# A second pair of value projections in seven half-sized products, its rows put in order through DRAM

## The chip, the cores and the metric

The kernel runs on one core of one Trainium2 chip. The metric is the time of one execution on the device in microseconds (us); lower is better. A time is the median of several runs; the traces come from one profiled execution each.

## The reference

One layer of a decoder trunk, in float32, for 512 tokens of width 1024. What matters here is the first half, the mixer:

```python
proj = x @ w_in        # (512,1024) @ (1024,9216): q/k/v of three branches and three gates
o_da  = diff_attention(...)            # 4 heads, values da_v: 512 columns, keys in order
o_sb  = stick_breaking_attention(...)  # 8 heads, values sb_v: 512 columns
o_dl  = dilated_attention(...)         # 3 groups x 4 heads, dilation 1, 4 and 16
# values dl_v[0], dl_v[1], dl_v[2]: 512 columns each, for the three groups
merged = sum_i sigmoid(gate_i) * (o_i @ w_branch_i)
x = layer_norm(alpha * x + merged @ w_out)
# then a squared-ReLU MLP and a gated per-layer embedding, and a second layer norm
```

The first dilated group (dilation 1) and the differential attention read their values in the order of the tokens; the second and third dilated groups read every fourth token, so that for them the rows stand in four classes (token number modulo 4).

## The kernel before

**Products.** Each operand is held as two float32r tiles, a rounded high part and the rest (h and l), and a product is three matmuls: h by h, h by l and l by h. The weights stream from DRAM in chunks of 128x1024 float32 (512 KB). A chunk is loaded on the SP queue into one of six raw buffers (line 211), cast to its high part by ACT (line 243), and its low part is a subtraction on DVE (line 245). Six pairs of h and l buffers make the ring; chunks are split up to six ahead of the matmuls, and a chunk's buffers come free when its last matmul is done.

**Items.** All projections stand in one list `items`, in an order that `main_order()` gives. A T item (line 292) makes 128 columns of q or k, transposed, with one chunk and 24 matmuls of 128x512. A V projection (`v_items`, line 488) makes 512 value columns in four items of 24 matmuls each, one for each 128 tokens, with four chunks in all; its four results are copied to SBUF by DVE (line 513). The rows are in the order of the tokens.

**Seven products.** A pair of value projections (`value_pair`, line 441) is a product of a 2x2 block matrix of tokens by input rows with a 2x2 block matrix of weights. It is computed with seven block products in place of eight (the scheme of Strassen and Winograd, p = 1 to 7), each as two half-sized items of 12 matmuls. Products 1, 2 and 3 take the activations as they are: their stationary operand reads every fourth column of `xh` and `xl` (line 364, `2 * th + r::4`), so that the rows come out in classes. Products 4 to 7 take sums of activation blocks, which `value_forms` makes on DVE and splits on ACT and DVE, from a copy of x that is loaded on the POOL queue. On the weight side they take sums of weight chunks. These are made in DRAM by DMA with an accumulating add on the POOL queue (`sum_steps`, lines 1095 and 1097), ahead of time, a few steps for each item: every item adds `size * rate` to a credit, and each whole credit issues one step. Up to four chains of steps run in turn, and a step of a chain needs the one before it landed. Two sums of a pair, for products 7 and 3, are made in place by `then_add`: a DMA on the POOL queue adds a second block onto the raw chunk after it was split for another product (line 176).

**Order around the change.** Behind the stick-breaking items (numbers 0 to 10) come the q and k items of dilated head 0 (11 to 16), two items of head 1, the plain value projection `dl_v` 0 (19 to 22), the other four items of head 1, the six of head 2, the pair `dl_v` 1 and 2 (33 to 46), the plain projection `da_v` (47 to 50), then the q and k of the differential heads and of dilated head 3, up to item 64. The gate and branch products follow, then the output projection and the MLP, all with their own weight sums.

**Attention pieces.** The attention heads are generators. `step()` (line 1937) is called at every item, and once more in the middle of a T or V item, and moves each active head on by one piece: some small matmuls and then work on ACT and DVE. The eight stick-breaking heads go first, two at a time, then dilated heads 0, 1 and 2, and so on. A dilated head ends with its product with the values (lines 1905 and 1910), which needs all three `dl_v`; a differential block needs `da_v` (line 1751). Semaphores are set by the framework from the tiles that an instruction reads and writes; the order of an engine's instructions is in the main the written one, but the framework may put a ready instruction ahead of one that it expects to wait.

Of the kernel before, what the change touches and what calls it, by code (L numbers as in the profile page):

```python
# [10 lines left out]
F32 = mybir.dt.float32  # L11
# [5 lines left out]
S = 512  # L17
# [18 lines left out]
def main_order():  # L36
# [5 lines left out]
    for h in range(4):  # L42
        for g in range(3):
            o += [("T", "dl_q", 4 * g + h), ("T", "dl_k", 4 * g + h)]
            if h == 1 and g == 0:
                o += [("V", "dl_v", g)]
        if h == 2:
            o += [("V", "dl_v", 1), ("V", "dl_v", 2), ("V", "da_v", 0)]
# [7 lines left out]
def trunk(tc, a, out):  # L56
    nc = tc.nc
    es = ExitStack()
    with es:
# [306 lines left out]
        vsum = [[dram.tile([P, 1024], F32, name=f"vsum{m}_{i}") for i in range(2)] for m in range(2)]  # L366
        v_from = [None]

        def load_xr():

            r = {}
            for h in range(2):
                for th in range(2):
                    for kp in range(2):
                        t = slot("xr")
                        i = nc.gpsimd.dma_start(t.rearrange("p (k t) -> p k t", k=2),
                                                xt[:, 4 * h + 2 * kp:4 * h + 2 * kp + 2, 256 * th:256 * th + 256])
# [10 lines left out]
        def value_forms():  # L388

            xr = [slot("xr") for _ in range(8)]  # L390
            for k, t in enumerate(xr):
                i = nc.gpsimd.dma_start(t, xt[:, k, :])
                tc.add_manual_dep(getattr(i, "ins", i), lows[-1].name, mybir.DependencyInfo(
                    mybir.DependencyClass.Sync, mybir.DependencyReason.DATA), reason="not ahead of time")

            def blk(kh, k, th):
                return xr[4 * kh + k].rearrange("p (t c) -> p c t", c=4)[:, 2 * th:2 * th + 2, :]

            def new():
                ts = [slot("fr") for _ in range(2)]  # L400
                return ts, [ts[k // 2].rearrange("p (k c t) -> p k c t", k=2, c=2)[:, k % 2] for k in range(4)]

            def parts(p, ts):
                form(vf, p, ts)
                vf[p] = [[(h[:, r * P:r * P + P], lo[:, r * P:r * P + P]) for r in range(2)] for h, lo in vf[p]]

            def neg_sub(o, i, j):
                nc.vector.scalar_tensor_tensor(o, i, -1.0, j, op0=OP.mult, op1=OP.subtract)

            for _ in range(WAIT):  # L410
                yield
            f7, o7 = new()
            with tc.issue_after(st["low"]):
                for k in range(4):
                    nc.vector.tensor_sub(o7[k], blk(1, k, 1), blk(0, k, 1))
            parts(7, f7)
            yield
            f6, o6 = new()
            with tc.issue_after(st["low"]):
                for k in range(4):  # L420
# [1732 lines left out]
```

## Time and profile before

| | |
|---|---|
| median of 3 runs | 1042.92 us (1042.3 to 1043.47) |
| the profiled execution | 1043.19 us |
| its span in the trace | 1041.0 us |
| granted TensorE clock | 0.998 |
| DMA traffic | 249.21 MB, mean 239 GB/s |

The trace's views are read so: the page gives for each engine the time in which at least one of its instructions was in flight. TensorE's matmuls overlap (a 128x512 matmul shows 389 ns, while the next one starts earlier), so the price of a matmul is the distance between two starts and not its duration. The view of windows gives the busy time of each engine in a stretch of the span, with the share of time that the 16 DMA engines were busy. The timeline lists instructions by start.

### The profile page before, as it was taken

The numbers are of one execution on the slowest core, as the hardware profiler recorded it, in microseconds if no ns is written. First come the engines' busy times: TensorE is split into PE (matmuls) and PEld (weight loads), VectorE is DVE, ScalarE is ACT, GpSimd is POOL, SyncE is SP. The second block draws the span as 40 slices with busy tenths as digits, with TensorE's granted clock in tenths as the row PEclk, the third lists the DMA queues.
The fourth block names the chain that finished last, engine by engine and source line by source line (L and its number), as shares of the span: only waits on it lengthen the run. The fifth ranks groups of instructions, "written<-read, shape, count | busy, mean of one in ns | idle before, by whom it ended". The sixth has DMA issues, their size and how long they took to land.

```text
span 1041.0 us, 15056 instructions
## 1 busy us (share of the span) xinstructions
PE 1031.1 (99%) x5450; PEld 880.1 (85%) x5450; DVE 787.0 (76%) x1408; ACT 593.2 (57%) x1014; POOL 180.0 (17%) x271
## 2 busy tenths in 40 slices
PE   9999999999999999999999999999999999999997
PEld 6888788889888888888888888889999889889886
DVE  6888577769774667779788895798768877877966
ACT  7566445536344545676575743775666556555651
POOL 0003412031211232411011040111111111111001
PEclk9999999999999999999999999999999999999999
DMA  8449978495985999967889795479999999999612
GB/s 308 121 154 271 255 214 197 128 283 142 278 207 206 258 281 294 248 199 202 251 238 230 269 320 197 147 219 331 320 288 316 296 316 314 306 344 286 201 59 81
DMA packets 71323, 249.21 MB, mean 239 GB/s; under 512 B 8809, under 2 KB 9593, under 8 KB 71249
## 3 DMA queue, kind: packets, MB, share of 16 engines
q0 software_dynamic: 32464, 116.21, 44.7%
q1 hardware_dynamic: 38208, 131.13, 35.2%
q8 instruction: 43, 0.70, 0.3%
q10 hardware_dynamic: 576, 0.92, 0.2%
q14 instruction: 32, 0.25, 0.1%
HBM read 246.10 MB, written 98.59 MB: 331 GB/s over the span
## 4 chain that ended last, share of the span: by engine, by line
PE 94%; DVE 2%; ACT 2%; issue 1%; DMA 0%; POOL 0%; DVEq 0%; POOLq 0%
PE mm L87 10%; PE mm L88 10%; PE mm L89 10%; PE at L1261 4%; PE at L1262 4%; PE at L1263 4%; PE at L599 3%; PE at L601 3%; PE at L600 3%; PE mm L496 2%; PE mm L498 2%; PE mm L497 2%; PE at L89 1%; PE at L87 1%; PE at L88 1%; PE at L761 1%
## 5 line engine op out<-in xcount | busy, mean ns | idle before, releaser
L243 ACT CAST wh<-raw 128x1024 fp32r<-128x1024 f32 x257 | 268.7, 1049 | 241.1 <-PE mm L88 133.6
L245 DVE TENSOR_TENSOR wl<-raw,wh 128x1024 fp32r<-128x1024 f32 x257 | 312.5, 1222 | 112.2 <-ACT wh L243 110.9
L87 PE MATMUL mm<-xhT,wh 128*128 128x512 f32 x302 | 120.0, 397 | 0.0
L89 PE MATMUL mm<-xhT,wl 128*128 128x512 f32 x302 | 118.3, 392 | 0.0
L88 PE MATMUL mm<-xlT,wh 128*128 128x512 f32 x302 | 118.2, 391 | 0.0
L87 PE MATMUL mm<-x1hT,wh 128*128 128x256 f32 x256 | 73.8, 288 | 0.0
L1261 PE MATMUL at<-wh,hh 128*128 128x512 f32 x188 | 73.7, 392 | 0.0
L1262 PE MATMUL at<-wl,hh 128*128 128x512 f32 x188 | 73.7, 392 | 0.0
L1263 PE MATMUL at<-wh,hl 128*128 128x512 f32 x188 | 73.1, 389 | 0.0
L88 PE MATMUL mm<-x1lT,wh 128*128 128x256 f32 x256 | 72.2, 283 | 0.0
L89 PE MATMUL mm<-x1hT,wl 128*128 128x256 f32 x256 | 71.8, 283 | 0.0
L89 PEld LDWEIGHTS mm<-xhT,wl 128*128 128x128 f32 x302 | 56.8, 188 | 12.0
L87 PEld LDWEIGHTS mm<-xhT,wh 128*128 128x128 f32 x302 | 56.8, 188 | 11.3 <-issue 0.4
L88 PEld LDWEIGHTS mm<-xlT,wh 128*128 128x128 f32 x302 | 56.8, 188 | 10.5
L87 PEld LDWEIGHTS mm<-x1hT,wh 128*128 128x128 f32 x256 | 48.8, 190 | 4.8 <-ACT up L1195 2.9
L88 PEld LDWEIGHTS mm<-x1lT,wh 128*128 128x128 f32 x256 | 48.9, 191 | 1.5
L89 PEld LDWEIGHTS mm<-x1hT,wl 128*128 128x128 f32 x256 | 48.6, 191 | 0.0
L1095 POOL DMA_DIRECT2D usum<-in_wu_dram x32 | 28.5, 928 | 103.1 <-DVE wl L245 38.7
L1095 POOL DMA_DIRECT2D dsum<-in_wd_dram x28 | 25.5, 933 | 100.2 <-DVE wl L245 33.3
L1263 PEld LDWEIGHTS at<-wh,hl 128*128 128x128 f32 x188 | 35.3, 188 | 7.6
L1261 PEld LDWEIGHTS at<-wh,hh 128*128 128x128 f32 x188 | 35.5, 189 | 6.0
L1262 PEld LDWEIGHTS at<-wl,hh 128*128 128x128 f32 x188 | 35.5, 189 | 5.6
(601 smaller groups left out, 2686.4 us busy)
## 6 DMA issues: line engine op xcount, KB each, us to landing
usum<-in_wu_dram POOLq DMA_DIRECT2D x48, 512.0 KB, 9.2
dsum<-in_wd_dram POOLq DMA_DIRECT2D x42, 512.0 KB, 9.1
raw<-in_wt_dram SPq DMA_DIRECT2D x38, 512.0 KB, 5.7
raw<-usum SPq DMA_DIRECT2D x32, 512.0 KB, 7.8
raw<-dsum SPq DMA_DIRECT2D x28, 512.0 KB, 8.1
raw<-in_wd_dram SPq DMA_DIRECT2D x25, 512.0 KB, 6.5
raw<-in_wu_dram SPq DMA_DIRECT2D x24, 512.0 KB, 7.2
raw<-in_wv_dram SPq DMA_DIRECT2D x18, 512.0 KB, 5.5
```

What stands on the lines that cost most here:

```text
L87: nc.tensor.matmul(ps, wh, xh, start=start, stop=False, skip_group_check=True)
L88: nc.tensor.matmul(ps, wh, xl, start=False, stop=False, skip_group_check=True)
L89: nc.tensor.matmul(ps, wl, xh, start=False, stop=stop, skip_group_check=True)
L243: i = nc.scalar.copy(h, raw)
L245: i = nc.vector.tensor_sub(lo, raw, h.bitcast(F32))
L599: nc.tensor.matmul(ps, h[:, q], c["h"][:, n], start=go, stop=False, skip_group_check=True)
L600: nc.tensor.matmul(ps, h[:, q], c["l"][:, n], start=False, stop=False, skip_group_check=True)
L601: nc.tensor.matmul(ps, lo[:, q], c["h"][:, n], start=False, stop=end, skip_group_check=True)
L1095: i = nc.gpsimd.dma_start(o, i, accum_op=OP.add, max_dma_last_dim=4096)
L1261: nc.tensor.matmul(ps, h[:, q], c["h"][:, s], start=go, stop=False, skip_group_check=True)
L1262: nc.tensor.matmul(ps, h[:, q], c["l"][:, s], start=False, stop=False, skip_group_check=True)
L1263: nc.tensor.matmul(ps, lo[:, q], c["h"][:, s], start=False, stop=end, skip_group_check=True)
```

## The change

The plain projections `dl_v` 0 and `da_v` become a second pair, computed in the same seven products as `dl_v` 1 and 2. `value_quad` lists the 28 half-sized items of both pairs; each product is done for pair q=0 and then for q=1, and both use the same forms of x. The four projections now stand together behind the q and k items of dilated head 1 (items 23 to 50); the items of head 2, of the differential heads and of head 3 follow (51 to 70).

- The rows of the second pair come out in classes, but are needed in order. Each of its eight result tiles is written by a DMA on the POOL queue into a DRAM tensor (`to_rows`), and four tiles each of `dl_v` 0 and `da_v` are read back in order (`from_rows`), also on the POOL queue, at items 53 and 60.
- Only product 7's weight sum is still made with `then_add`, for both pairs. Product 3's is a third sum in DRAM: four chains of six steps in place of two chains of four.
- x for the forms comes from a second input, `xR`, in which the classes are contiguous, and the forms are made in place in fewer, larger DVE instructions.
- The credits of the sum steps are set anew: they start at item 7 and not 12, pause at items 18 to 22, and run at 0.45 a half-sized item and 3.2 a T item behind the pairs (before 0.3 and 2.6); the output projection's items have 2.0 and the MLP's items 0.62 (before 1.0 and 0.6).
- The tables of the differential heads are loaded at item 52 in place of 44.

```diff
     for h in range(4):
         for g in range(3):
             o += [("T", "dl_q", 4 * g + h), ("T", "dl_k", 4 * g + h)]
-            if h == 1 and g == 0:
-                o += [("V", "dl_v", g)]
+        if h == 1:
+            o += [("V", "dl_v", 1), ("V", "dl_v", 2), ("V", "dl_v", 0), ("V", "da_v", 0)]
         if h == 2:
-            o += [("V", "dl_v", 1), ("V", "dl_v", 2), ("V", "da_v", 0)]
             for d in range(2):
                 o += [("T", "da_q", d), ("T", "da_k", d)]
...
+            r11, r12, r21, r22 = load_xr(a["xR"])
...
+            for _ in range(WAITS[0]):
+                yield
             with tc.issue_after(st["low"]):
+                for kp in range(2):
+                    nc.vector.tensor_sub(r22[kp], r22[kp], r12[kp])
+            parts(7, r22)
...
+        WAITS = (5, 6, 4, 4)
+        plain_rows = [dram.tile([S, 512], F32, name=f"rows{n}") for n in range(2)]
+
+        def to_rows(n, c, t):
+            nc.gpsimd.dma_start(plain_rows[n].rearrange("(i c) d -> c i d", c=4)[c], t)
+
+        def from_rows(n, name):
+            for tt in range(4):
+                V[name, 0, tt] = t = slot(name)
+                nc.gpsimd.dma_start(t, plain_rows[n][tt * P:tt * P + P, :])
+
+        def value_quad(nv):
+
+            v_from[0] = len(items) - 2
...
+            for p, q in ((1, 0), (1, 1), (7, 0), (7, 1), (2, 0), (2, 1), (6, 0), (6, 1), (4, 0), (4, 1),
+                         (5, 0), (3, 0), (5, 1), (3, 1)):
                 for r in range(2):
                     if not r:
+                        cs[p, q] = [then_add(cs[1, q][kp], w[q][kp][2]) if p == 7 else
+                                    chunk(w[q][kp][blk[p]] if p in blk else vsum[q][kp][{5: 0, 6: 1, 3: 2}[p]], 1024)
+                                    for kp in range(2)]
...
+                    def put(n, c, t, q=q):
+                        if q:
+                            to_rows(n, c, t)
+                        else:
+                            V["dl_v", 1 + n, c] = t
...
+                    items[-1]["rate"] = 0.9
+            v_end[0] = len(items)
...
-                if name != "dl_v" or j == 0:
+                if name == "sb_v":
                     v_items(nv, name, j)
-                elif j == 1:
-                    value_pair(nv)
+                elif (name, j) == ("dl_v", 1):
+                    value_quad(nv)
...
-            it.setdefault("rate", 2.8 if j < 25 else 0.0 if j < 31 else 2.6)
+            it.setdefault("rate", 2.6 if j < 18 else 0.0 if j < 23 else 3.2)
...
+                    items[-1]["rate"] = 2.0
...
-            todo = deque(two_steps(vsum[m], [w[2 + i // 2, i % 2 * 2 + m] for i in range(4)], True)
-                         for m in range(2))
+            todo = deque(some_steps(vsum[q][m], [w[1 + 2 * q + i // 2, i % 2 * 2 + m] for i in range(4)], True)
+                         for q in range(2) for m in range(2))
...
-            while any(("dl_v", g, 3) not in V for g in range(3)):
+            while any(("dl_v", g, t) not in V for g in range(3) for t in range(4)):
                 yield
...
-        DA_TABS = 44
+        DA_TABS = 52
...
+            if n == v_end[0] + 2:
+                from_rows(0, "dl_v")
+            if n == v_end[0] + 9:
+                from_rows(1, "da_v")
...
-            if 12 <= n < wout_at + 8:
+            if 7 <= n < wout_at + 8:
                 credit += it["size"] * it.get("rate", 1.0)
             elif n > ple_at + 6:
-                credit += 0.6
+                credit += 0.62
```

130 lines of the change are left out of this document (57 added, 73 removed).

## The prediction

> **What bounds the kernel now.** I read the page's head, the chain of waits and the table of slices first, then the windows view.
>
> ```profile
> span 1041.0 us, 15056 instructions
> PE 1031.1 (99%) x5450; PEld 880.1 (85%) x5450; DVE 787.0 (76%) x1408; ACT 593.2 (57%) x1014; POOL 180.0 (17%) x271
> PEclk9999999999999999999999999999999999999999
> ...
> PE 94%; DVE 2%; ACT 2%; issue 1%; DMA 0%; POOL 0%; DVEq 0%; POOLq 0%
> ...
> 25.00:900.00 875.00, 873.73 (x4581) 745.02 (x4580) 665.37 (x1226) 502.36 (x875) 162.59 (x239) 1.00 0.83 243
> ```
>
> The program's time was 1043.19 us in this execution: the span of 1041.0 and 2.2 around it. TensorE (PE) is busy for 1031.1 us of it and makes 94% of the chain of waits; from 25 to 900 us it idles for 875.00 - 873.73 = 1.3 us. Its clock is full in all slices. So the time is PE's work, laid end to end, and a change pays what it takes from PE unless it makes PE wait. Removing stalls can win 1.3 us at most. The DMA engines (0.83) and DVE (665 of 875 us) are well used too: these are what the change loads.
>
> The price of a matmul has to be read from starts, not from durations. In the timeline of PE, the first and last rows of an unbroken run of 24 matmuls of product 6 (contiguous operand), of 24 of product 3 (every fourth column), and of 21 of a plain value item:
>
> ```profile
> 257.72 0.39 PE L465 MATMUL mm<-wh,u6h 128*128 128x512 f32 x1
> 262.93 0.39 PE L467 MATMUL at<-wh,u6l 128*128 128x512 f32 x1
> ...
> 275.75 0.40 PE L465 MATMUL at<-wh,xhT 128*128 128x512 f32 x1
> 281.16 0.39 PE L467 MATMUL at<-wh,xlT 128*128 128x512 f32 x1
> ...
> 160.45 0.39 PE L496 MATMUL mm<-wh,xhT 128*128 128x512 f32 x1
> 164.99 0.40 PE L498 MATMUL mm<-wh,xlT 128*128 128x512 f32 x1
> ```
>
> (262.93 - 257.72) / 23 = 0.2265 us, (281.16 - 275.75) / 23 = 0.2352 us, and (164.99 - 160.45) / 20 = 0.227 us. By the durations of 0.39 us one would expect nearly twice the gain.
>
> **The change part by part.**
>
> *Matmuls.* The two plain projections have 2 x 4 x 24 = 192 matmuls; a pair in seven products has 7 x 24 = 168. Of these, 96 (products 4 to 7) have contiguous operands and 72 (1 to 3) strided ones. Removed: 192 x 0.227 = 43.6 us. Added: 96 x 0.2265 + 72 x 0.2352 = 21.7 + 16.9 = 38.7 us. Net: -4.9 us, by 24 matmuls fewer (-5.4) and 72 that are slower by 0.008 us (+0.6).
>
> The strided operand has one more price, where an attention piece stands ahead of it:
>
> ```profile
> 242.55 0.60 PE L465 MATMUL at<-wh,xhT 128*128 128x512 f32 x1
> 242.99 0.40 PE L466 MATMUL at<-wl,xhT 128*128 128x512 f32 x1
> ...
> 266.57 0.47 PE L465 MATMUL at<-wh,u4h 128*128 128x512 f32 x1
> 266.88 0.39 PE L466 MATMUL at<-wl,u4h 128*128 128x512 f32 x1
> ...
> L465 PEld LDWEIGHTS at<-wh,xhT x16: 308/310/311, 242.5 to 280.5; 128*128 128x128 f32 x16
> L465 PEld LDWEIGHTS mm<-wh,u6h x4: 187/188/188, 257.5 to 259.5; 128*128 128x128 f32 x4
> ```
>
> After a piece of small matmuls the first interval is 0.44 us strided and 0.31 contiguous, 0.20 and 0.08 over the steady ones. In the written order 11 strided half-items now start behind a piece, where 3 did before; the pieces themselves are the same, so 8 x 0.12 = +1.0 us. PE's work: -4.9 + 1.0 = -3.9 us.
>
> The weight load of a strided operand takes 310 ns and not 188, longer than the 0.235 us from start to start: the load is hidden for the most part. Were it to set the distance, the 72 would cost 72 x 0.310 = 22.3 us and the pair would save nothing (21.7 + 22.3 = 44.0 against 43.6); the run of 24 at 0.2352 speaks against it. The Trainium skill (TensorE: Matmul & The Clock Gate, "Back-to-back issue gap" and "LDWEIGHTS") says that load and matmul set the distance together, and that a load takes its columns over 1.2 GHz: an estimate of 107 ns for 128 columns, by which the operand's stride would cost nothing at all. The trace's 188 and 310 ns differ from it, and the measurement decides.
>
> *DVE in the pairs.* The busy groups of DVE, and its load in a stretch of T items (second half of the stick-breaking heads), in the old pair, and in `da_v`:
>
> ```profile
> L245 DVE TENSOR_TENSOR wl<-raw,wh 128x1024 fp32r<-128x1024 f32 x56 | 68.3, 1222 | 32.6 <-ACT wh L243 32.1
> L1635 DVE TENSOR_TENSOR spl<-e,sph 128x512 fp32r<-128x512 f32 (+1 forms) x24 | 15.6, 648 | 0.9
> L1675 DVE TENSOR_TENSOR al<-a,ah 128x512 fp32r<-128x512 f32 (+1 forms) x24 | 15.5, 648 | 1.0
> L1631 DVE SCALAR_TENSOR_TENSOR e<-at,e 128x512 f32<-128x512 f32 (+1 forms) x24 | 15.5, 645 | 15.5 <-ACT e L1630 15.3
> L1634 DVE CAST sph<-e 128x512 fp32r<-128x512 f32 (+1 forms) x24 | 9.8, 410 | 0.9
> L1674 DVE CAST ah<-a 128x512 fp32r<-128x512 f32 (+1 forms) x24 | 9.8, 407 | 2.7 <-ACT a L1671 2.6
> L1693 DVE TENSOR_TENSOR oT<-at,ot 64x512 f32<-64x512 f32 x8 | 5.4, 681 | 2.8 <-ACT ot L1692 2.7
> L484 DVE SCALAR_TENSOR_TENSOR dl_v<-dl_v,at 128x512 f32<-128x512 f32 x3 | 2.0, 682 | 0.4 <-PE at L467 0.4
> ...
> 148.84 0.34 PE L1661 MATMUL at<-sph,tri_r 128*128 128x384 f32 x1
> 150.24 0.40 PE L496 MATMUL mm<-wh,xhT 128*128 128x512 f32 x1
> 246.28 0.41 PE L1841 MATMUL at<-r,fold 128*128 128x32 f32 x2
> ...
> 175.00:200.00 25.00, 25.00 (x123) 20.67 (x122) 16.39 (x28) 13.05 (x21) 0.80 (x1) 1.00 0.68 178
> 237.60:281.40 43.80, 43.72 (x207) 39.32 (x206) 37.04 (x87) 22.89 (x41) 7.87 (x11) 1.00 0.71 193
> 283.00:325.00 42.00, 42.00 (x251) 36.93 (x250) 25.53 (x110) 16.15 (x45) 4.88 (x7) 1.00 0.69 176
> ```
>
> A pair has 14 chunks where two projections have 8: 6 x 1.222 = 7.3 us more for DVE, and 12 evictions of 0.68 on DVE (products 2, 4, 5, 3 one, product 6 two, for each half) where there were 8: 2.7 us. ACT gets 6 casts and 4 copies more; it has 16 to 24 us of work in 42 to 44, and nothing hangs on it. The forms, 16 instructions of half size before, become 8 of 128x512, and both pairs share them. On the whole DVE has room: 25.53 of 42 us in `da_v`. But the place matters. Counting steps, the last two and a third stick-breaking heads fall into the first 18 half-items of the pairs, where before they lay in T items (16.39 of 25 us). There DVE has 18 low parts (22 us), about 14 evictions (9.6), the forms (8 sums and 8 splits of 0.68: 11), and 2.3 heads of at least (15.6 + 15.5 + 15.5 + 9.8 + 9.8 + 5.4) / 8 = 9 us (21): 64 us. PE has 18 x 12 x 0.23 = 50 us, and for each head some four pieces like the one from 148.84 to 150.24 (1.4 us): 2.3 x 5 = 12, together 62. So DVE is at its limit for some 60 us. It falls 2 us behind, or 7 with the smaller instructions of a head, which I left out (some 2 us each). The cover: chunks are split six ahead, six half-items of 2.8 us, so that the low parts may be 10 us late; the evictions have two banks and six. I take +0.5 us, bounds 0 and +7 (all that it falls behind), nearest to 0 because the old pair ran PE for 43.72 of 43.80 us beside 85% of DVE.
>
> *Sums and loads.* SP gets 24 chunk loads for 18 (6 more); POOL gets 24 sum steps for 8, 8 writes and 8 reads of rows, and as many `then_add` as before (4).
>
> ```profile
> q0 software_dynamic: 32464, 116.21, 44.7%
> q1 hardware_dynamic: 38208, 131.13, 35.2%
> ...
> 324.20:425.70 101.50, 101.36 (x517) 84.62 (x516) 65.60 (x189) 52.58 (x124) 31.50 (x46) 1.00 0.99 277
> ...
> xr<-in_xT_dram POOLq DMA_DIRECT2D x16, 256.0 KB, 8.0
> xn<-in_xn_dram POOLq DMA_DIRECT2D x8, 256.0 KB, 10.5
> out_dram<-xn SPq DMA_DIRECT2D x4, 256.0 KB, 2.0
> ...
> DMA to landing us min/median/max: 7.4/8.6/11.3
> ...
> 431.67 0.71 POOL L376 DMA_DIRECT2D xr<-in_xT_dram  x1 [1.86 <-DMA dsum<-in_wd_dram]
> L562 DVE TENSOR_TENSOR xr<-xr,xr x2: 682/684/686, 442.4 to 443.1; 128x512 f32<-128x512 f32 x2
> ```
>
> POOL's queue took 44.7% of 1041 = 465 us of the 16 engines for 116.21 MB, 4.0 us a MB or 2.1 for a step; SP's 2.8 a MB or 1.5 for a load. So the DMA engines get 16 x 2.1 + 6 x 1.5 + 16 x 1.05 = 60 us more, against some 0.17 x 875 = 150 idle. They are mostly free while the stick-breaking heads run and in the pairs (0.71 in the old one); but items 51 to 64 already had them at 0.99. There the new rate is 3.2 for 2.6: 20 T items with 20 x 24 x 0.2265 = 109 us of matmuls and 45 of pieces (101.5 - 76 = 25 in the window from 324.20, which is items 51 to 64, and 42 - 22 = 20 of the dilated heads, which ran beside `da_v` from 283) would issue 64 steps, 20 loads and 20 half-sized loads: 134 + 30 + 21 = 185 us in 154. POOL must fall up to 30 us behind there and make it up in the branch and gate products. (In the pairs a write of rows waits on POOL for its eviction, with at most one sum step for two half-items queued behind it; nobody waits for these soon. The tables of the differential heads, issued at item 52, are turned by DVE at 56, 4 x 5.4 us later, and land in 8.6: 13 to spare.) The sums are due later than that: by the credits 105 steps stand at the end of the T items where 80 are needed for everything before the MLP (90 and 64 before), so the lead is the same. What could notice is x for the gates' forms, loaded on POOL behind these steps: its last issue was at 431.67 and DVE used it at 442.4. I take 0, bounds 0 and +8 (that use late by some 20 us, less the six chunks ahead).
>
> *Rows through DRAM.* The last `dl_v` rows leave with product 3 of the second pair (item 50). After its end: eviction 0.7, a write (2.0 for the store to the output of the same size, 8 if it fares like POOL's other DMAs), four reads issued in 2 to 3 us, and landing in 7.4 to 11.3: 12 to 23 us. Heads 0 and 1 use them at item 53, two T items and some pieces later: 48 x 0.2265 = 10.9 us and more. So PE would wait 1 to 12 us if it kept the written order. It need not: items 53 to 56 use no values, 22 us of matmuls, and the row at 246.28 above is a head's piece (L1841) put between two matmuls of product 2, so the order follows what is ready. `da_v` has ten items of cover. I take 0, bounds 0 and +12, since the 22 us are near to all that is needed.
>
> The Trainium skill (DMA: Bandwidth & Descriptors, "Anatomy of one DMA — SWDGE (gpsimd) path") fits a GpSimd DMA by 2.0 us and its bytes by 436 GB/s: an estimate of 2.6 us for 256 KB, by which the rows would be there after 9 us and never late. The rows above (8.0, 8.6 and 10.5 us) are three to four times that on these busy queues, and I go by them.
>
> **Sum.** 1043.19 - 3.9 + 0.5 = 1039.8 for this execution; the median of the runs shown, 1042.92, lies 0.3 lower, so 1039.5.
>
> **The rivals.**
> - *Rows late (slower).* PE keeps the written order, or the framework expects the reads too early, and PE stands at the first product of head 0 with `dl_v` 0 (L1905). For: the reads lie behind sum steps on POOL in the densest stretch, where landing is longest; 8 us of wait are in reach. Against: the 22 us of other work. It decides from 3.4 us of wait on, and can be measured from 5.5; at 8 the time is 1047.5. A POOL queue that is late for the gates' x would look the same in the sum.
> - *DVE eats it (no change).* In the pairs PE waits for low parts or banks for 3 us: 1042.3. For: 64 to 69 us of DVE beside 62 of PE. Against: the six chunks of lead, and free DVE time in the T items behind.
> - *The loads bind (no change).* The 72 strided matmuls cost their loads' 0.310 and not 0.2352: 72 x 0.075 = +5.4, so 1044.9. Against: 24 in a row held 0.2352.
>
> **How the numbers follow.** About 0.2% (2.1 us) is what a measurement of this kernel can tell from no change: faster means under 1040.8, slower over 1045.0. The forecast, with up to 1.8 us of waits, has 0.58. DVE's waits of 2 to 5.5 us have 0.12 and binding loads 0.03: no change, 0.15 together. Rows or POOL late by 5.5 us or more have 0.27. The low end is PE's -4.9 with no start price, and some 0.5 of the idle: 1037.5. The high end takes in most of the late rows: 1047.5. The likeliest case alone spans 1037.5 to 1041.
>
> **What would show it.** Right: about 24 matmuls fewer; PE's idle from 25 to 900 us still under 3 us; L465's successor at 0.235 us strided; DVE over 90% in the first pairs' half and PE not waiting for it; the DMA share at 1.0 for the items behind the pairs. Wrong: a gap of PE at L1905 or L1751 ended by a DMA; DVE waiting for x of the gates; PE idle in the pairs for low parts; intervals of strided matmuls above 0.25.

## The result, and the profile after

The changed kernel takes 1081.19 us (median of 6 runs, 1080.01 to 1082.8), the kernel before 1042.81 on the same chip: a ratio of 1.0368, 95% interval 1.0355 to 1.0381. It is 38 us slower, where 3.4 us of gain were forecast. The page's head and its chain of waits, as shown of before:

```profile
span 1080.1 us, 15136 instructions
PE 1036.4 (96%) x5426; PEld 884.4 (82%) x5426; DVE 792.7 (73%) x1410; ACT 601.0 (56%) x1024; POOL 201.0 (19%) x303
PEclk9999999998989989999999999999999999999999
...
PE 76%; issue 8%; DMA 8%; DVE 4%; ACT 2%; POOL 2%; DVEq 0%; POOLq 0%; ACTq 0%
```

The span is 39.1 us longer. PE is idle for 1080.1 - 1036.4 = 43.7 us (9.9 before), which makes 33.8 of it, and busy for 5.3 us more, although it runs 24 matmuls fewer (5426 for 5450). The chain has DMA, DVE and "issue" in it now, and the row of clocks is no longer all nines. Where PE stood, from the view of waits (engine and line, what ended the wait, us in total, times, longest):

```profile
PE at L1761 <- DMA da_v<-rows: 10.3, 1, 10.3
PE at L1915 <- DMA dl_v<-rows: 7.4, 1, 7.4
PE at L1694 <- DVE ah L1684: 5.2, 3, 4.0
PE at L1696 <- DVE al L1685: 4.6, 2, 4.4
PE at L1671 <- DVE sph L1644: 2.5, 2, 2.2
```

Two long waits for rows from DRAM (17.7 us), at the differential blocks' and the dilated heads' products with the values, and some 12.3 us in the pairs, for tiles of the stick-breaking heads: ah and al (the high and low part of the weights) and sph (the high part of an earlier step). Nothing waits for a raw chunk. The windows view, one stretch in the pairs and one behind them (PE, weight loads, DVE, ACT and POOL busy, clock, DMA share, GB/s):

```profile
210.00:250.00 40.00, 28.58 (x116) 22.47 (x115) 29.88 (x45) 15.29 (x22) 3.05 (x5) 0.91 0.51 158
290.00:350.00 60.00, 52.64 (x266) 44.30 (x265) 19.34 (x55) 16.34 (x33) 18.18 (x30) 0.94 1.00 299
```

In the first, PE works for 28.58 of 40 us. DVE is busy for 29.88, so it isn't full there. In the second the DMA share is 1.00.

Idle time costs twice. In PE's timeline of the changed kernel, at the longest gap and behind it (start, duration, engine, line, operation, and idle before):

```profile
389.89 0.76 PE L1761 MATMUL at<-da_v,wT 128*128 128x128 f32 x2 [10.35 <-DMA da_v<-rows]
...
391.95 0.63 PE L88 MATMUL mm<-xhT,wl 128*128 128x512 f32 x1
392.38 0.63 PE L86 MATMUL mm<-xhT,wh 128*128 128x512 f32 x1
...
393.16 0.39 PE L88 MATMUL mm<-xhT,wl 128*128 128x512 f32 x1
393.39 0.40 PE L86 MATMUL mm<-xhT,wh 128*128 128x512 f32 x1
```

The windows view of 10 us each around it (PE, weight loads, DVE, ACT, POOL, clock, DMA share, GB/s):

```profile
380.00:390.00 10.00, 0.10 (x1) 0.14 (x1) 2.43 (x5) 2.42 (x6) 4.46 (x8) 0.64 1.03 311
390.00:400.00 10.00, 10.00 (x49) 8.67 (x50) 1.91 (x3) 2.81 (x8) 4.15 (x5) 0.85 1.03 268
```

At 391.95 the starts lie 0.43 us apart, and only from 393.16 on 0.23 again; the granted clock of the 10 us up to 390 is 0.64 and of the next 10 us 0.85 (the last column but two). With the 3.8 us that the matmuls really win (shown below), slow matmuls make 5.3 + 3.8 = 9.1 us for 33.8 us of idle: 0.27 us for each us of waiting. The expectations below use 0.28. This is an average of one kernel and not a rate. In windows of half a us the clock is at half for 3.4 us behind the gap of 4.0 us, for 6.8 around each of those of 4.4 and 7.4, and for 10.2 around the longest. PE is busy for 3.5, 5.6, 5.0 and 3.6 us of these four stretches and loses half of that: 8.9 us, nearly all of the 9.1. So a gap of 10 us costs no more clock than one of 4 (1.8 us each), and a short one can cost none: behind a gap of 2.15 us at 234 us the clock stayed full.

### The profile page after: what moved, and what is told of

It reads as the page before. It is cut to its first block, busy times and chain, and to the rows that moved or that the text cites. A ratio compares the mean times of both kernels' runs of the same rounds, so it can differ in the third digit from the quotient of the medians.

```text
span 1080.1 us, 15136 instructions
## 1 busy us (share of the span) xinstructions
PE 1036.4 (96%) x5426; PEld 884.4 (82%) x5426; DVE 792.7 (73%) x1410; ACT 601.0 (56%) x1024; POOL 201.0 (19%) x303
## 4 chain that ended last, share of the span: by engine, by line
PE 76%; issue 8%; DMA 8%; DVE 4%; ACT 2%; POOL 2%; DVEq 0%; POOLq 0%; ACTq 0%
PE mm L86 8%; PE mm L87 8%; PE mm L88 8%; PE at L1271 4%; PE at L1272 4%; PE at L1273 4%; PE at L606 3%; PE at L607 3%; PE at L608 3%; PE at L88 1%; PE at L86 1%; PE at L87 1%; DVE wl L244 1%; DMA usum<-in_wu_dram 1%; DMA rows<-dl_v 1%
## 5 line engine op out<-in xcount | busy, mean ns | idle before, releaser
L244 DVE TENSOR_TENSOR wl<-raw,wh 128x1024 fp32r<-128x1024 f32 x263 | 319.7, 1221 | 132.5 <-ACT wh L242 130.7
L242 ACT CAST wh<-raw 128x1024 fp32r<-128x1024 f32 x263 | 275.0, 1049 | 235.1 <-PE mm L87 128.3
L86 PEld LDWEIGHTS mm<-xhT,wh 128*128 128x128 f32 x302 | 57.2, 189 | 11.3 <-issue 0.4
L87 PEld LDWEIGHTS mm<-xlT,wh 128*128 128x128 f32 x302 | 57.1, 189 | 10.3
```

The source lines that it names most:

```text
L86: nc.tensor.matmul(ps, wh, xh, start=start, stop=False, skip_group_check=True)
L87: nc.tensor.matmul(ps, wh, xl, start=False, stop=False, skip_group_check=True)
L242: i = nc.scalar.copy(h, raw)
L244: i = nc.vector.tensor_sub(lo, raw, h.bitcast(F32))
```

## The experiments

**No rows through DRAM.** The second pair's result tiles are used as they are, in classes; this kernel leaves out the ordering of the rows:

```diff
-    to_rows(n, c, t)
+    V[("dl_v", "da_v")[n], 0, c] = t
```

> Leaves out the ordering of the rows: the second pair's eight result tiles are used as dl_v 0 and da_v straight from SBUF, in classes, with no writes to DRAM and no reads. All other work and its order are written as in the changed kernel. Theory A (the loss is PE standing at values late from DRAM, 7.36 + 10.34 us, and in the pairs at low parts and heads' tiles, 12.5 us, of which 2.60 and 4.91 us are waits for a slot that a write of rows still reads; and each us of idle costs some 0.28 us more by a lower clock, from +33.8 idle and +5.3 busy with 3.9 us of work less): the two gaps at L1915 and L1761 and those at L1671 and L1696 go, the one at L1694 (4.02) stays; 24.2 us of idle less, 24.2 x 1.28 = 31, so about 1050 us. Rival B (the denser sums keep the 16 DMA engines full, and everything that loads is late): only the two DRAM gaps go, others come near 310 and 390 us in their place, over 1065. Rival C (the place: DVE beside the stick-breaking heads is the larger part): the pairs keep over 10 us of gaps, 1058 or so.

Measured: 1051.6 us (ratio 1.0081, 1.0066 to 1.0096), so 29.6 of the 38 us hang on this trip. The longest of PE's waits in this run:

```profile
PE at L1694 <- DVE ah L1684: 4.5, 2, 4.0
PE mm L460 <- ACT u4h L270: 1.1, 1, 1.1
```

The two DRAM waits and the one at L1696 are gone, as theory A says; that at L1671 for sph falls from 2.5 to 0.3 us, and the 4.0 us at L1694 stay. The waits that went in the pairs were not for rows as data. They were for the SBUF slots of tiles whose rows a DMA still reads. In the changed kernel's trace, DVE's timeline:

```profile
247.13 0.69 DVE L1685 TENSOR_TENSOR al<-a,ah 128x512 fp32r<-128x512 f32 x1 [4.91 <-DMA rows<-dl_v]
```

and the waits of ACT in the pairs:

```profile
ACT e L1638 <- DMA rows<-dl_v: 2.6, 1, 2.6
```

DVE stood 4.91 us before it could write al, and ACT 2.6 us before e, until a write of rows had landed. The writer is not waiting for its own data: it was given the slot of a dl_v tile that had been sent off.

**Values used later; the rows on SP's queue; the sums paused.** Three runs on why the rows are late:

```diff
 # later use (reads of da_v at item 57 for 60; dl_v 0 used from item 55, not 53)
-    V[name, 0, tt] = t = slot(name)
+    held[name, 0, tt] = t = slot(name)   # entered in V some items later
 # SP's queue
-    nc.gpsimd.dma_start(... plain_rows ...)
+    nc.sync.dma_start(... plain_rows ...)
 # pause
+    if v_end[0] - 5 <= n < v_end[0] + 4:
+        pass                             # no credit for sum steps
+    # and from v_end + 4 to the last T item: credit += 1
```

> The rows go through DRAM as in the changed kernel, but more items lie between a read and its use: the dilated heads may use dl_v 0 two items later than now (the reads stay where they are), and da_v is read at three items ahead of its use (item 57, used from 60). Theory A: PE's fixed order is what makes the landing time visible; both gaps (7.36 and 10.34 us) go and nothing else changes: 17.7 x 1.28 = 22.7, so about 1058.5. Rival B (POOL's queue falls further behind the more it is given, so that the reads land later too): over 4 us remain at each place, 1068 or more. Rival D (the pieces of the heads that are pushed back take PE time at the end of the T items that nothing covers): the two gaps go, but the time stays over 1065 with new gaps behind item 64.

Measured: 1068.8 us (1.0254, 1.0215 to 1.0293). Both DRAM waits are gone, as theory A says, but a new one has come, of 7.0 us, at the gates' products. PE's waits, and the view of the tile x (xr), whose DMAs POOL issues:

```profile
PE mm L703 <- ACT b L709: 7.0, 1, 7.0
```

```profile
L376 POOL DMA_DIRECT2D xr<-in_xT_dram x8: 708/712/1060, 450.2 to 459.7; - x8
```

x for the gates' forms is issued from 450.2 to 459.7 us only, and PE stands for it until 469. Rival B's time came out, but not its place: no wait is left at the two products, and what comes late on POOL's queue is x. In the changed kernel x is issued even later (456.4 to 463.8 us), but PE's 17.7 us of standing had moved its first use to 478.8 us.

> The writes and reads of the rows are issued on SP's queue in place of POOL's; nothing else is changed. Theory A1 (it is POOL's queue that is slow for them: writes and reads wait there behind sum steps and their landings): the reads land 2 to 5 us after issue, the gap at L1915 falls from 7.36 to under 2 and that at L1761 from 10.34 to under 5, and tiles come free earlier in the pairs; 1060 to 1068. Theory A2 (any 256 KB transfer takes 7 us or more in this stretch because the 16 engines are full): the gaps stay over 5 and 8 us, within 5 us of 1081. Rival: the chunk loads queue behind SP's waits for evictions, and PE waits for raw chunks in the pairs: over 1085.

Measured: 1068.9 us (1.0249, 1.0234 to 1.0264). The wait at L1761 is gone and the one at L1915 stays (7.4 us at its longest). The view of the tile rows in this run shows why (line, queue, operation, durations in ns, first and last issue; landing for all its DMAs):

```profile
L432 SPq DMA_DIRECT2D dl_v<-rows x4: 326/376/424, 298.5 to 299.8; - x4
L432 SPq DMA_DIRECT2D da_v<-rows x4: 370/398/424, 358.6 to 360.0; - x4
DMA to landing us min/median/max: 2.3/11.3/16.4
```

and in the changed kernel:

```profile
L432 POOL DMA_DIRECT2D dl_v<-rows x4: 536/537/538, 297.8 to 305.2; - x4
L432 POOL DMA_DIRECT2D da_v<-rows x4: 836/842/875, 379.6 to 381.2; - x4
DMA to landing us min/median/max: 3.2/7.9/12.0
```

A DMA lands no sooner on SP: 11.3 us in the median against 7.9 (the writes alone 8.7 against 6.8). Theory A1's reason falls, and A2's forecast that both gaps stay falls too. What helped da_v is that SP runs ahead of PE and issued its reads at 358.6 us, some 20 us before their use, where POOL issues them at 379.6, when PE stands there already.

> No sum step is issued from item 46 to 54, around the writes and reads of dl_v 0; from item 55 to the end of the T items each item issues one more, so that the sums catch up. Theory A1 (the reads stand behind sum steps on POOL): they are issued as soon as the writes have landed, the gap at L1915 falls from 7.36 to about 3; that at L1761, which lies in the denser stretch now, grows to 11 to 14: 1077 to 1083. Theory A2 (PE's order places the use a fixed few us behind the write, and write plus read are longer than that on an idle queue too): over 5 us stay at L1915, 1080 to 1086.

Measured: 1076.8 us (1.0331, 1.0311 to 1.0351). With no sums beside them, the reads of dl_v 0 are issued from 294.0 to 295.6 us (297.8 to 305.2 before), land 5.6 us later in the median, and PE doesn't wait for them at all. In the denser stretch behind, da_v's take longer. PE's longest wait, and the landing in the view of the tile da_v:

```profile
PE at L1761 <- DMA da_v<-rows: 15.2, 1, 15.2
```

```profile
DMA to landing us min/median/max: 14.3/16.3/16.4
```

The gap at L1915 goes, further than A1 says, but the time is only moved: what the first rows won, the second ones lost. The pause takes the sums off POOL's queue and off the DMA engines at once, so this run doesn't tell the two apart. Nor does the DMA share: it is 1.00 from 294 to 302 us, where a read lands in 5.6 us, and 1.05 from 370 to 389, where it takes 16.3.

**x for the gates on SP's queue**, on top of the later values:

```diff
-    i = nc.gpsimd.dma_start(t ...)       # x of the gates' forms
+    i = nc.sync.dma_start(t ...)
```

> As the kernel with the values used later (1068.8 us), and x for the gates' forms, eight DMAs of 256 KB, is loaded on SP's queue in place of POOL's. Theory A (with the two DRAM gaps gone, PE reaches the gates earlier, and x, issued on POOL behind sum steps that wait for each other, comes 10.2 us late for DVE, which PE feels as 7.02 us before the product with oTh): this gap goes: 1068.8 - 7.0 x 1.28 = about 1060. Rival (the 16 engines are full, so that x or the chunks behind it on SP are late by as much): over 4 us of gap remain between 430 and 480 us, 1065 or more.

Measured: 1072.6 us (1.0268, 1.0233 to 1.0303), no better. x is issued from 433.8 us on, 16 us earlier, but lands late. PE's longest wait, and the landing in the view of the tile xr:

```profile
PE mm L703 <- ACT b L709: 12.2, 1, 12.2
```

```profile
DMA to landing us min/median/max: 9.7/24.2/35.4
```

24 us in the median. Theory A falls and the rival holds: it is not POOL's order that is short there, but DMA time.

**The place alone.** Only the first pair goes in seven products; dl_v 0 and da_v are plain projections behind it, in the same place, with no DRAM trip (the steps of the forms and the tables' item are moved to fit, not shown):

```diff
             for p, q in ((1, 0), (1, 1), ...):
+                if q:
+                    continue
...
-                if name == "sb_v":
-                    v_items(nv, name, j)
+                elif (name, j) != ("dl_v", 2):
+                    v_items(nv, name, j)    # sb_v, dl_v 0, da_v
```

> The place alone: the four value projections stand together behind the q and k items of dilated head 1, but only the first pair goes in seven products, with the contiguous x and the larger forms; dl_v 0 and da_v are plain projections of four items each behind it, with no rows through DRAM; the sum rates stay those of the changed kernel. PE's work is that of the kernel before. Theory A (the pairs beside the stick-breaking heads cost DVE's waits whichever they are): 3 to 6 us of gaps between 165 and 290 us, 1043 + 4 to 8 = 1047 to 1051. Rival (the place costs nothing; it is the second pair's chunks and slots that do): under 1.5 us of gaps there, 1043 to 1044.5. Rival (the faster sums): the gaps lie behind 290 us.

Measured: 1073.5 us (1.0294, 1.0266 to 1.0321), far from both. PE's longest waits in this run (L699 is the gates', the others lie in the pairs):

```profile
PE mm L699 <- ACT b L705: 18.2, 1, 18.2
PE at L1673 <- DVE sph L1646: 2.7, 1, 2.7
PE at L145 <- DVE oT L1705: 1.0, 1, 1.0
```

In the pairs these gaps and smaller ones come to some 5 us, as theory A says, without the second pair's chunks, slots or rows. But this kernel's whole V items bring 2.4 credits each where half-sized ones bring 0.45, so that more sum steps were issued by the gates, and x came 18.2 us late there. That was an oversight of the experiment; its total says nothing on the place, but it shows once more what the third resource is.

**What makes the 4 us at L1694.** In the timeline of the kernel without the DRAM trip (which the next three runs share), ACT's and DVE's rows ahead of that gap:

```profile
208.76 0.60 ACT L1681 ACTIVATE a<-at 128x512 f32<-128x512 f32 x1 [2.85 <-DVE al L1685]
...
210.32 1.23 DVE L244 TENSOR_TENSOR wl<-raw,wh 128x1024 fp32r<-128x1024 f32 x1 [1.66 <-ACT wh L242]
210.62 1.04 ACT L242 CAST wh<-raw 128x1024 fp32r<-128x1024 f32 x1 [0.34 <-PE at L462]
...
212.84 1.29 DVE L398 SCALAR_TENSOR_TENSOR xr<-xr,xr 128x512 f32<-128x512 f32 x2
214.05 0.42 DVE L1684 CAST ah<-a 128x512 fp32r<-128x512 f32 x1
...
214.61 0.47 PE L1694 MATMUL at<-ah,sb_v 128*128 128x512 f32 x1 [4.03 <-DVE ah L1684]
```

ACT has a ready at 209.36. DVE, in its order, first makes the low parts of two chunks (the first at 210.32), and the second's cast waits for PE itself to free the ring (210.62, <-PE at L462), then two sums for the forms, and only then ah, at 214.05. PE stands meanwhile, for something that stands behind other work in DVE's order; the wait for PE itself is a small part of it (0.34 us of the 4.03). Three edits were aimed at this order:

```diff
 # casts and low parts written one half-sized item later
-    pump(freed, ...)
+    pump(freed - lag, ...)
 # the forms' sums behind the newest al
-    with tc.issue_after(st["low"]):
+    with tc.issue_after(st["al"]), tc.issue_after(st["low"]):
 # heads 5 to 7: one step more ahead of the product with the values
+    if hd >= 5:
+        yield
```

> As the kernel without the ordering of the rows (1051.6 us; it leaves out that ordering), and in the 28 half-sized items the casts and low parts of the next chunks are written one half-item later. Theory A (at 214.61 PE waits 4.02 us for a head's ah, which DVE could have made from 209.4 on, but which stands in DVE's order behind two low parts whose casts wait for PE itself to free the ring): ah stands ahead of them now, the gap goes, and with its clock 4.0 x 1.28 = 5 us: about 1046.5. Rival (DVE has no time left beside the stick-breaking heads): PE waits for low parts in place of ah, the gaps from 180 to 290 us stay over 5 us together, 1050 to 1054.

> As the kernel without the ordering of the rows (1051.6 us; it leaves out that ordering), and the four sums of the forms for products 6 and 5 (about 0.65 us each) are put behind the newest al on DVE. Writing casts and low parts later (the run before) had left DVE's order as it was: two low parts and four sums stay ahead of ah. Theory A (DVE's order, not its amount of work, makes the 4.02 us): ah moves ahead by 4 x 0.65 = 2.6 us, the gap at L1694 shrinks to about 1.4, 1051.6 - 2.6 x 1.28 = about 1048. Rival (DVE's amount): PE waits for the forms of product 6 in place of ah, the sum of the gaps from 165 to 290 us stays at 6 us or more, 1050.5 or more.

> As the kernel without the ordering of the rows (1051.6 us; it leaves out that ordering), and the stick-breaking heads 5, 6 and 7 wait one step (two half-sized items, some 5.5 us of matmuls) longer between their weights' high and low parts and the product with the values. Theory A (PE asks for ah 4 us too early for DVE's order, in which it stands behind two low parts that wait for PE): the gap at L1694 goes altogether and none over 1 us comes in its place: 1051.6 - 4.0 x 1.28 = about 1046.5. Rival (DVE's amount of work in this stretch is the limit): PE waits elsewhere from 165 to 290 us, over 5 us in sum, 1050 or more.

Measured: 1050.8, 1054.3 and 1050.1 us. The first two were inconclusive: in their traces the two low parts and two sums still come ahead of ah, with gaps of 4.03 and 4.25 us (the second also has 5.0 us for x at the gates). In the second run the two casts follow each other without a wait for PE, and the gap is there all the same. The framework may order instructions by times that it expects, and these two shifts in the written order didn't move them. The third moved PE's request instead: the gap at 214 us is gone, but head 7 now meets the same pattern at 242 us, with 3.98 us. By its numbers alone the rival (DVE's amount of work) would have held; the last runs below decide.

**All waits taken out, one by one, with the rows through DRAM.** On top of the later values: the sum steps at other rates; the sent tiles held longer by a copy of one element, which gives e and al other slots; the steps for heads 5 to 7, and one more for head 7.

```diff
-    items[-1]["rate"] = 0.9              # half-sized items
+    items[-1]["rate"] = 1.6              # then 1.3 (1.1 in the last run)
-    2.6 if j < 18 else 0.0 if j < 23 else 3.2
+    2.6 if j < 20 else 0.0 if j < 23 else 2.5   # then 2.7 (2.8)
...
+    while keep and clock[0] - keep[0][1] >= 10:
+        t = keep.popleft()[0]
+        ...
+        nc.vector.tensor_copy(kept, t[0:1, 0:1])
```

One ACT-queue variant came first, with the writes of rows on ACT's queue, x on SP's and the lagged casts:

> All of it together: values used later, x for the gates on SP's queue, casts and low parts one half-item later in the pairs, and the eight writes of rows on ACT's queue (the reads stay on POOL's). Theory A (a head's e and al wait 2.6 and 4.9 us for an SBUF slot that a write of rows still reads, 6.8 us in the median from issue to landing on POOL's queue): on a queue with nothing else in it the writes land in 2 to 4 us, and with the lag the gaps in the pairs are under 3 us together: 1060 - 5 - 6 x 1.28 = about 1048. Rival (ACT stands in order at each write until DVE has evicted the tile, and the casts behind it are late): PE waits for low parts in the pairs, 1053 or more.

Measured: 1072.1 us (1.0273, 1.0252 to 1.0295). The slot waits stay (4.7 us at al), and x is late by 11 us. The writes land in 5.8 us in the median on a queue of their own, 6.8 on POOL's in the changed kernel: theory A's 2 to 4 us was wrong.

> As the kernel with the values used later (1068.8 us), with the sum steps spread otherwise: 1.6 in place of 0.9 for the pairs' items (0.8 a half-sized item), no pause at items 18 and 19, and 2.5 in place of 3.2 behind the pairs; the number of steps by the end of the T items is within two of before. Theory B' (behind the pairs the 16 DMA engines are full, DMA share 1.02 to 1.03 from 290 to 450 us; the two DRAM gaps had given them 22 us more time, and without these gaps x for the gates is late by 7 to 12 us on either queue): 14 steps of some 2.1 us of the 16 engines' time less there is 29 us; x is in time, the gap at L703 is under 1 us: about 1060, and no gap comes in its place. Rival (x is late for a slot or another reason): 5 us or more stay at L703, 1066 or more. Rival (the steps take their time in the pairs now): PE waits there for raw chunks or forms, by more than the 10.5 us of gaps of that kernel.

Measured: 1067.6 us (1.0236, 1.0221 to 1.0251). x is in time and the DMA share from 350 to 450 us is 0.88 in place of 1.01; but the sums run beside the writes of rows now. Two of PE's waits:

```profile
PE at L1677 <- DVE sph L1650: 6.4, 2, 6.1
...
PE at L1921 <- DMA dl_v<-rows: 3.2, 1, 3.2
```

The wait at sph, 1.5 us at its longest in the run with later values, is 6.1 here, and the rows of dl_v 0 are late by 3.2 us again. The cause of the x gap was right, and the forecast that nothing comes in its place was wrong.

> All that has been found: values used later, sum steps spread as in the run beside this one, the forms' sums behind the newest al, and each tile whose rows are written to DRAM held ten steps longer (by a copy of one element), so that the slots of the heads' e and al are others, with no write to wait for. Theory: of 1068.8 us go 7.0 x 1.28 for x, 2.6 x 1.28 for the order on DVE and 6 x 1.28 for the slots: about 1049. Rival (the slots only move the wait: SBUF is full, so some other tile is late): 3 us or more of new gaps in the pairs, 1053 or more.

Measured: 1058.4 us (1.0147, 1.013 to 1.0164). The slot waits at sph and al are gone, so that was their cause. 4.2 us at ah and 3.5 at the rows remain, and the time is 9 us above the theory's.

> With the rows through DRAM as in the changed kernel: one step more for heads 5 to 7, written tiles held ten steps longer, dl_v 0 used four items later and da_v read three items ahead of its use, and the sum steps at 1.3 for the pairs' items and 2.7 behind them. Theory: of the 1058.4 us of the version with later values, held tiles and spread sums go 4.2 us at ah and 3.5 us at the rows of dl_v 0, with their clock 7.7 x 1.28 = 10: about 1048.5; no version comes below the 1043 of before unless PE's other 3 us (starts of strided items, slow clock) go too. Rival (DMA time is the limit: with fewer sums moved forward x for the gates is late again, with more the rows are): 3 us or more at L1921 or L703, 1053 or more.

Measured: 1049.0 us (1.0061, 1.0047 to 1.0075), as the theory says. Of the long waits only head 7's is left, and the timeline of this run shows the pattern once more:

```profile
238.36 0.39 PE L471 MATMUL at<-wh,u4l 128*128 128x512 f32 x1
...
238.90 1.04 ACT L242 CAST wh<-raw 128x1024 fp32r<-128x1024 f32 x1
...
239.85 0.96 ACT L1690 ACTIVATE a<-at 128x384 f32<-128x384 f32 x2
240.25 1.22 DVE L244 TENSOR_TENSOR wl<-raw,wh 128x1024 fp32r<-128x1024 f32 x1
...
242.25 0.42 DVE L1693 CAST ah<-a 128x512 fp32r<-128x512 f32 x1
...
242.73 0.49 PE L1705 MATMUL at<-ah,sb_v 128*128 128x512 f32 x1 [3.98 <-DVE ah L1693]
```

Behind PE's last matmul (238.36) the cast of a chunk (238.90, 1.04 us) goes first on ACT, a behind it, the low part (240.25, 1.22) goes first on DVE, then ah, and PE starts 4 us later.

> As the version before (1049.0 us, rows through DRAM and all edits), with one more step for head 7 alone, so that PE has 24 matmuls (5.5 us) more between the weights' last sums and the product with the values. The 3.98 us there are the chain from PE's last matmul of product 4 by the cast (1.05) and the low part (1.23) of the chunk that it frees to a's two halves on DVE. Theory A (order): the gap goes and none over 1.3 us is left: 1049.0 - 4.0 x 1.28 = about 1044, against 1042.5 to 1043.2 of before: not faster, since some 2 us of small waits and slow starts remain of the 3.9 us that the matmuls win, and then some. Rival (amount): 3 us or more of gaps come elsewhere from 215 to 290 us, 1047.5 or more.

Measured: 1045.8 us (1.003, 1.0019 to 1.0042; 1043.75 to 1047.55). The gap is gone and nothing of that size came in its place. DVE makes ah at nearly the same time as before (242.54 us for 242.25), but PE asks for it only at 244.43. So the 4 us were a matter of order, not of amount.

> As the last version (1045.8 us), with dl_v 0 used five items after its reads are issued in place of four. Theory (the spread of 3.8 us from run to run is the landing of the rows): the gap at L1926 (0.28 + 0.71) goes, the runs lie within 1.5 us of each other and the median at the lowest of before this edit, about 1043.7. Rival (the spread is that of the chunk loads or of x for the gates): the median stays within 1 us of 1045.8 and the spread over 2.5 us.

> As the run beside it, with the sum steps at 1.1 in place of 1.3 for the pairs' items and 2.8 in place of 2.7 behind them. Theory (the rows' landing is all): no further gain, within 1 us of the run beside it. Rival (DMA time is still short behind the pairs): x for the gates comes late again, a gap of 1 us or more before the gates' products, 1045 or more; or, if it is short in the pairs, a gain of 1 us or more.

Measured: 1043.0 us (1.0003, 0.9994 to 1.0011; 1042.88 to 1043.65) and 1043.5 (1.0005, 0.9996 to 1.0014). The spread went with the rows' landing, and thinner sums beside the writes changed nothing. The first of them is the best version found: no different from the kernel before. Its page's head:

```profile
span 1041.2 us, 15151 instructions
PE 1027.3 (99%) x5426; PEld 878.4 (84%) x5426; DVE 789.8 (76%) x1418; ACT 600.2 (58%) x1024; POOL 202.2 (19%) x303
```

PE's longest wait:

```profile
PE mm L469 <- DVE dl_v L485: 1.3, 1, 1.3
```

and two of its windows, with the columns of above:

```profile
210.00:250.00 40.00, 38.73 (x177) 32.35 (x177) 37.44 (x59) 20.55 (x27) 7.43 (x12) 1.00 0.86 270
290.00:450.00 160.00, 159.17 (x833) 134.47 (x832) 97.11 (x301) 79.90 (x191) 50.07 (x75) 1.00 1.01 285
```

PE's work is 3.8 us less than before (1027.3 for 1031.1), all rows go through DRAM, DVE is busy for 37.44 of 40 us and PE doesn't wait for it longer than 1.3 us at a time; the DMA share behind the pairs is still 1.01. The gain of 3.8 us is eaten by 2.1 us more of gaps over 0.1 us (3.3 against 1.1 from 20 us on) and by 1.9 us more at the end of the program. PE's last matmul in the kernel before, and in this version:

```profile
1033.45 0.28 PE L1364 MATMUL at<-wh,hl 128*128 128x256 f32 x1
...
1031.70 0.28 PE L1383 MATMUL at<-wh,hl 128*128 128x256 f32 x1
```

PE is done 1.75 us earlier, but the span goes on for 9.2 us behind it (to 1041.2) and not for 7.3 (to 1041.0). The last write of the output is issued 3.9 us behind the last matmul in both, so the 1.9 us come behind that. No run was made on it. Over the runs the end grows with the DMAs issued on POOL's queue: 7.3 and 7.2 us with 250 and 252 of them (the kernel before, and the place alone), 7.6 to 8.2 with 266 (rows written on ACT's queue, rows on SP's, no rows through DRAM), 9.2 to 9.3 with 282 (the changed kernel and this version). Whether they are the cause isn't shown.

## Why the prediction was wrong, by its steps

- *Matmuls: right.* 24 fewer. In the pairs the steady intervals are 0.24 us strided and 0.23 contiguous (medians of starts that are given to 0.01), as taken, and in the version without waits PE has 3.8 us less work against 3.9 forecast. Strided loads don't bind.
- *Rows through DRAM: this step failed.* Of its two reasons the first, that PE's order "follows what is ready", is wrong for a landing that the framework misjudges: PE's order is fixed before the run, and PE went to L1915 behind items 51 and 52 and stood there, with T items queued behind it that needed nothing. With the reads on SP it went there even sooner (it stood there from 300.3 us on, not from 302.6), though they took longer to land. The second, "`da_v` has ten items of cover", mistook the write for the read. The ten items lie between the eviction and item 60, but the reads are issued at item 60, on the queue, at 379.6 us, and the block takes its values at once; the whole landing (10.3 us in the median) is bare. That was to be read in the diff, and cost more (10.3) than the part that was priced (7.4). The landing time itself, 12 to 23 us behind item 50, was right at its upper end: PE leaves item 50 at 286.6 us and has the rows at 310.0.
- *The write as a reader.* The prediction asked who waits for the rows, not who waits for the tiles that they are sent from. A DMA that reads a tile holds its slot until it lands, and the next owner waits.
- *DVE in the pairs: mis-sized.* +0.5 was taken with bounds of 0 and +7; without slot waits the gaps in the pairs were 6.3 us. The amounts were near (DVE is busy for 37.44 of 40 us there in the best version, and PE hardly waits). The cover was wrong: chunks six ahead help PE's own low parts, but a head's ah needs its place in DVE's order, and there it stood behind two low parts and two sums for 4 us.
- *Sums and loads: taken at 0, and hidden.* In the changed kernel nothing waits for x, because PE stands 17.7 us ahead of it. Without that, and with the rows still through DRAM, x makes PE wait 7.0 us, or 12.2 on SP's queue; the bound of +8 was near, the value 0 was luck. With no rows through DRAM, x is issued from 435.8 us on and PE doesn't wait for it.
- *The clock: not in the sum at all.* Every us of idle was counted as one.
- *The end of the program: not in the sum.* It is 2 us longer in the changed kernel (9.3 us behind PE's last matmul for 7.3).
- *The rivals.* "Rows late" was the right side and place, at 0.27; its price (8 us) left out da_v, the slots and the clock. "DVE eats it" took place as well. "The loads bind" did not.

By the runs the 38.4 us of loss are: some 22 for the bare landings (17.7 of waits and 4.3 of slow clock), about 9 for slots (12.3 us of waits in the pairs against 6.3 without the trip, and 2.8 of slow clock), 8 for DVE's order and small waits in the pairs (6.3, and 1.7 of slow clock), 2 for the end and some 2 for small waits elsewhere, less the 3.8 won: 39. The shares are not quite apart, since one wait gives time to the next.

That SP's queue made no transfer quicker, and ACT's the writes by 1 us only, is in line with the Trainium skill (DMA: Bandwidth & Descriptors, "Issuing engines are not separate DMA queues"): by it DMAs of all queues run on the same 16 engines and interleave, and another queue saves only the time to issue. The traces agree in the main: the eight writes land in 8.7 us on SP, 5.8 on ACT and 6.8 on POOL, the reads in 11.2 and 14.3 us on SP and 9.4 and 10.3 on POOL.

## What to carry to other kernels

Count a transfer's cover from where it is issued to where an engine first needs it in that engine's own fixed order, and list who waits for the tile that it reads as well as for the one that it writes. When a wait goes, ask what it had been paying for: here two stalls had given a full set of DMA engines the time to bring the next operand. A saving of 0.4% in matmuls is lost to a few waits of about 1 us and a longer end of the program, even where no wait is long enough to lower the clock.

## What was not expected of the hardware

- After 10.3 us of idle PE ran at half its rate (0.43 us between starts and not 0.23) until 3.3 us behind the gap, and gaps of some 4 us had the same effect (granted clock 0.91 from 210 to 250 us in the changed kernel, 1.00 in the best version, whose gaps there are 1.3 us at most). No gap of 1.5 us or less lowered the clock in any run, every gap of 2.6 us or more did; of two near 2.1 us, the one with the writes on ACT's queue did (2.08) and the one in the changed kernel didn't (2.15). The Trainium skill has this (TensorE: Matmul & The Clock Gate, "Part 1: The HAM clock gate"): PE's clock falls to half after an idle window of about 3.4 us and comes back after as long a busy one. The traces agree with the half rate and with the length (the stretches at half clock last 3.4 us or a multiple of it), but here gaps of 2.1 to 3.2 us were enough. The prediction did not use it.
- A 256 KB read that lands in 5.6 us beside no sums took 16.3 us in the median beside the denser ones, and eight reads of x, issued on SP's queue behind the pairs, 24 us. The DMA share was 1.00 to 1.05 in all three stretches: a share of 1 doesn't tell how late a transfer will be.
